# Left-factor sums of 35 block products built in DRAM by accumulating DMAs instead of on VectorE

## The chip, the cores and the metric

The kernel runs on one core of one Trainium2 chip. The metric is the device time of one execution in microseconds; a lower time is better. Three runs of the kernel before gave 2456.99, 2461.78 and 2462.23 us, median 2461.78. One more execution was recorded by the hardware profiler; it took 2457.39 us on the device, and the trace of it spans 2455.6 us.

## The reference, cut to what matters

One pre-norm layer on a sequence of 1024 rows of width 1024, in float32, then a last norm. Cut to its data flow:

```python
h = rmsnorm(x)
u = h @ w_in                      # 1024 x 11264, cut into dq, dk, dv, rq, rk, rv, rg, lx, ly, gates
od = diff_attention(dq, dk, dv)   # 8 heads, two softmaxes each, causal
o_r = silu(rg) * group_norm(retention(rq, rk, rv))
o_l = rg_lru(lx) * gelu(ly)       # convolution, gates, a scan over time
g = sigmoid(gates)                # three gates of width 1024
merged = g[0] * (od @ w_branch[0]) + g[1] * (o_r @ w_branch[1]) + g[2] * (o_l @ w_branch[2])
x = x + merged @ w_out
x = x + cross_attention(rmsnorm(x), rmsnorm(mem))
x = x + square(relu(rmsnorm(x) @ mlp_w1)) @ mlp_w2
return rmsnorm(x)
```

## The kernel before, in words

Every matmul operand is split into a high and a low part (`split`, lines 68 to 72: ScalarE writes the rounded high part, VectorE or GpSimd subtracts it for the low part), and one product is three matmuls (`mm3`, lines 57 to 61). So each operand costs a pass of ScalarE and one of VectorE or GpSimd before TensorE can use it.

The stages follow each other: retention (to about 262 us in the trace), attention (to about 740), `h_products` (to about 1220), three calls of `branch` (to about 1490), w_out and cross-attention, and the two matrix products of the MLP.

The products with `rg`, `lx` and `ly`, most of `gates`, the three w_branch matrices and mlp_w1 are made by a Strassen-like scheme with seven block products in place of eight (Winograd's form). Two rows of blocks of the left factor (here the weights) form a *pair*: `A11 A12` lie in one 128x1024 unit in DRAM, `A21 A22` in the next. The seven left operands are A11, A12, A22 and four sums, S1 = A21 + A22, S2 = S1 - A11, S3 = A11 - A21, S4 = A12 - S2 (`LEFT`, line 1058). The right operands are B11, B21, B22 and T1 to T4, which are made once and kept in SBUF as split blocks. There are 35 such pairs from the attention's end to the end of the third branch: 4 of `rg`, 8 of `lru`, 11 of `gate` in `h_products`, and 12 in the branches. mlp_w1 has 16 more, which the change leaves as they are.

For each pair `raw_pair` loads the two units on the SyncE queue (SP), `left` makes the four sums with four VectorE instructions of 128x512 (line 1066), in place over the loaded blocks, and `product` (lines 1103 to 1137) does the seven products of 12 matmuls each: `pair_unit` splits the left operand (ScalarE, then GpSimd or VectorE), the product goes into one PSUM bank, and VectorE adds the seven results up in the running sums `t0` and `t1` (lines 1125, 1127 and 1130) and in `emit`. The in-place sums must wait until the splits that read the old blocks are done. `h_products` and `branch` have six PSUM banks for these products (`p6`). In `h_products` the work of the LRU (convolution, line 615; scan, line 640) and the right-factor sums of the branches (`o_sums`, lines 739 to 750) run on the same VectorE queue.

In the attention stage each of the 8 heads has 8 steps of scores, softmax, transposes and products with v; the projections of the next heads fill in between. Their weights come through `weight` (lines 83 to 92): a 512 KB load on SP into one of three staging tiles, the high part on ScalarE, the low part on GpSimd, into one of four tiles `w`. The half of each q tile that lies on the other partitions is written by a DMA from SBUF to SBUF on the SP queue (`qd<-qd`, line 443), which the head's scores wait for.

The Python code writes the instructions in program order; a list scheduler puts them into one in-order queue for each engine, so an instruction can stand earlier or later than in the code. `after(key, ins)` chains instructions of one key in program order ("wdma" for weight loads, "wsplit" for their high parts). Each DMA on a queue also takes one of eight completion semaphores in turn.

Of the kernel before, what the change touches and what calls it, by code (L numbers as in the profile page):

```python
# [17 lines left out]
P = 128  # L18
# [31 lines left out]
class Kernel:  # L50
# [85 lines left out]
    def setup(self):  # L136
# [231 lines left out]
    def h_sums(self, kt, half, hp):  # L368
# [13 lines left out]
        for o, a, b in ((T2, B22, T1), (T4, B21, T2)):  # L382
            self.after("ret", tt(o, a[0], b))
            tt(o, o, a[1], ALU.add)
        nc.sync.dma_start(self.hTs[:, :, kt, c].rearrange("i p c -> p i c"), t[:, 0:4, :])
# [159 lines left out]
    def attention(self):  # L545
        self.vd, self.qkd, self.am = {}, {}, {}
        for _ in self.diff_v(0):
            pass
# [15 lines left out]
        for h in range(8):  # L564
# [25 lines left out]
        self.hp = self.h_products()  # L590
        for f in late:
# [55 lines left out]
    def h_products(self):  # L647
# [11 lines left out]
        sums = {4: [(0, 0)], 6: [(1, 0), (1, 1)], 8: [(1, 2), (1, 3)], 10: [(0, 1), (0, 2)], 12: [(0, 3)],  # L659
                14: [(2, 0), (2, 1)], 18: [(2, 2)], 20: [(2, 3)]}  # L660

        def run(p, k):
# [6 lines left out]
            elif kind == "rg":  # L669
                units = [a["w_rg"][2 * n + i] for i in range(2)]  # L670
            else:
                units = [a["w_gate"][self.gate_order[n + i]] for i in range(2)]

            def emit(i, j, x, y):
# [22 lines left out]
            psum = (lambda: self.ps.tile([P, HB], F32, tag="mm", name="ps1")) if k == 1 and p < 2 else None  # L697
            self.pair(p, k, c, units, H, psum or self.p6(sps), emit, nc.gpsimd)
            if kind == "lru" and k == self.ORDER[5]:
# [8 lines left out]
            if k == self.ORDER[2]:  # L708
                for i, q in sums.get(p, ()):
                    self.o_sums(i, q, sp)  # L710
# [28 lines left out]
    def o_sums(self, i, q, sp):  # L739
# [6 lines left out]
        (b11, b12), (b21, b22) = ([x[:, j, :] for j in range(2)] for x in t)  # L746
        for o, x, y in ((b11, b12, b11), (b12, b22, b12), (b22, b22, b11), (b21, b21, b22)):
            nc.vector.tensor_tensor(o, x, y, op=ALU.subtract)
        for e in range(2):
            nc.sync.dma_start(dst[2 * e:2 * e + 2, :, q, :].rearrange("i p c -> p i c"), t[e])  # L750

    def o_in(self, i):
# [39 lines left out]
    def branch(self, order, i, right, bw, st, sps, nxt):  # L792
# [25 lines left out]
        def run(p, k):  # L818
            units = [self.a["w_br"][i * 8 + 2 * p + e] for e in range(2)]
            self.pair(p, k, cs[p], units, right, self.p6(sps), lambda e, j, x, y: emit(2 * p + e, j, x, y),  # L820
                      v if k in (6, 4) else nc.gpsimd)
# [259 lines left out]

    def pair(self, p, k, c, units, right, psum, emit, lo):
# [5 lines left out]
        if "left" not in c and 1 in c and 2 in c:  # L1088
            c["left"] = True
            w = c["w"]  # L1090
            self.left(w, self.sf[:, 4 + p % 2, :], w["A11"], w["A12"], self.nc.vector)
        self.product(k, c, right, psum, lo, emit)

# [8 lines left out]

    def product(self, k, c, right, psum, lo, emit):

# [21 lines left out]
        if ready("u3", 7, "u2"):  # L1126
            v.tensor_tensor(t1, c[7], t0, op=ALU.add)
        if ready("c22", 5, "u3"):
            emit(1, 1, c[5], t1)
            v.tensor_tensor(t0, c[5], t0, op=ALU.add)  # L1130
        if ready("c21", 4, "u3"):
# [152 lines left out]
    def run(self):  # L1284
        tc, nc, a = self.tc, self.nc, self.a
        pool = lambda name, bufs=1, side="right", **kw: tc.tile_pool(name=name, bufs=bufs, side=side, reuse_waits="tile", **kw)
        self.setup()
        with pool("slotA", bufs=4, side="left") as self.slotA:
            self.n_gates, self.gate_order = 0, [b * 8 + n for b in (1, 0, 2) for n in range(8)]
# [108 lines left out]
```

## Time and profile before

| | |
|---|---|
| runs, median (lowest to highest) | 2461.78 us (2456.99 to 2462.23) |
| profiled execution, device time | 2457.39 us |
| its span in the trace | 2455.6 us |
| TensorE (PE) busy | 2320.9 us, 95% |
| weight loads of TensorE (PEld) busy | 1908.8 us, 78% |
| VectorE (DVE) busy | 1854.2 us, 76% |
| ScalarE (ACT) busy | 1044.8 us, 43% |
| GpSimd (POOL) busy | 1091.8 us, 44% |
| DMA, moved | 338.28 MB, mean 138 GB/s |

In the profile an engine's row gives busy time, not useful time: matmuls are pipelined, and a busy TensorE at a lower granted clock (PEclk) does less. "A <- B" among the waits reads: A's engine sat idle until B had ended. PE rows count matmuls; at full clock 88 to 90 matmuls of 128x512 fit into 20 us. L numbers are lines of the kernel before.

### The profile page before, as it was taken

How to read it: one execution, taken by the hardware profiler on the slowest of the kernel's cores; microseconds unless marked ns; L12 is line 12 of the kernel's file. 1: busy time of each engine (PE TensorE's matmuls, PEld its weight loads, DVE VectorE, ACT ScalarE, POOL GpSimd, SP SyncE). 2: the span in 40 equal slices, each digit the busy share in tenths (PEclk: the TensorE clock that was granted, in tenths of full speed). 3: DMA queues.
4: the chain of work that ended last, by engine and by line, in shares of the span. 5: the costliest groups of instructions: out<-in, count | busy, mean ns of one | idle time of the engine just before them, and what ended most of it. 6: DMA issues, size and time to landing. Idle time of an engine off the chain costs nothing. (4 is left out here: it accounts for less than half of the span.)

```text
span 2455.6 us, 31231 instructions
## 1 busy us (share of the span) xinstructions
PE 2320.9 (95%) x11132; PEld 1908.8 (78%) x11132; DVE 1854.2 (76%) x2850; ACT 1044.8 (43%) x1823; POOL 1091.8 (44%) x714
## 2 busy tenths in 40 slices
PE   9999999999998999999998987999989999999996
PEld 7888878888876877777876766788768888778884
DVE  7677387877786776786677898345788888788888
ACT  5444355555545454445244443135432222343333
POOL 1122212221216555566542334034155555698787
PEclk9999999999999999999999988999999999999999
DMA  4222222222225345453676776343325444734431
GB/s 170 80 86 70 65 61 69 66 64 62 61 56 195 119 162 171 140 178 112 208 252 211 256 263 193 112 162 104 106 80 175 150 156 141 274 138 172 158 138 74
DMA packets 137259, 338.28 MB, mean 138 GB/s; under 512 B 17152, under 2 KB 27393, under 8 KB 137104
## 3 DMA queue, kind: packets, MB, share of 16 engines
q1 hardware_dynamic: 136528, 334.44, 41.4%
q8 instruction: 89, 1.46, 0.2%
q10 hardware_dynamic: 576, 1.84, 0.2%
q14 instruction: 66, 0.54, 0.1%
HBM read 229.21 MB, written 98.63 MB: 134 GB/s over the span
## 5 line engine op out<-in xcount | busy, mean ns | idle before, releaser
L59 PE MATMUL ps<-block,wu 128*128 128x512 f32 x1428 | 570.7, 400 | 53.8 <-DVE sf L1125 21.5
L61 PE MATMUL ps<-block,wu 128*128 128x512 f32 x1428 | 567.8, 398 | 11.4 <-POOL wu L71 6.2
L60 PE MATMUL ps<-block,wu 128*128 128x512 f32 x1428 | 564.4, 395 | 1.7 <-POOL block L71 1.0
L71 POOL TENSOR_TENSOR wu<-st,wu 128x512 fp32r<-128x512 f32 x214 | 323.3, 1525 | 317.5 <-ACT wu L70 317.4
L59 PEld LDWEIGHTS ps<-block,wu 128*128 128x128 f32 x1428 | 272.9, 191 | 118.1 <-issue 19.5
L61 PEld LDWEIGHTS ps<-block,wu 128*128 128x128 f32 x1428 | 272.8, 191 | 79.2 <-POOL wu L71 11.0
L60 PEld LDWEIGHTS ps<-block,wu 128*128 128x128 f32 x1428 | 272.9, 191 | 62.8 <-DVE block L71 1.6
L70 ACT CAST wu<-st 128x512 fp32r<-128x512 f32 x240 | 141.2, 618 | 166.6 <-DVE st L1066 71.3
L71 POOL TENSOR_TENSOR w<-st,w 128x1024 fp32r<-128x1024 f32 x50 | 123.7, 2485 | 158.3 <-ACT w L70 158.2
L59 PE MATMUL ps<-wu,hu 128*128 128x512 f32 x448 | 177.2, 395 | 17.1 <-DVE acc L1198 14.3
L61 PE MATMUL ps<-wu,hu 128*128 128x512 f32 x448 | 174.8, 392 | 3.6 <-DVE hu L71 3.6
L60 PE MATMUL ps<-wu,hu 128*128 128x512 f32 x448 | 175.5, 392 | 0.0
L1198 DVE TENSOR_TENSOR acc<-acc,ps 128x512 f32<-128x512 f32 x216 | 137.8, 678 | 20.4 <-PE ps L61 19.9
L71 POOL TENSOR_TENSOR wu<-sf,wu 128x512 fp32r<-128x512 f32 x63 | 116.7, 1866 | 67.9 <-ACT wu L70 57.3
L71 DVE TENSOR_TENSOR hu<-sth,hu 128x1024 fp32r<-128x1024 f32 x56 | 121.1, 2167 | 20.9 <-ACT hu L70 20.2
L466 ACT ACTIVATE p<-sc,mx 128x256 f32<-128x256 f32 (+7 forms) x128 | 94.8, 741 | 71.1 <-DVE mx L463 49.2
L59 PEld LDWEIGHTS ps<-wu,hu 128*128 128x128 f32 x448 | 84.7, 189 | 41.3 <-DVE acc L1198 12.4
L61 PEld LDWEIGHTS ps<-wu,hu 128*128 128x128 f32 x448 | 84.7, 189 | 22.6 <-DVE hu L71 4.9
L59 PE MATMUL psk<-block,w 128*128 128x512 f32 x256 | 101.7, 397 | 0.0
L61 PE MATMUL psk<-block,w 128*128 128x512 f32 x256 | 101.2, 395 | 0.0
L60 PE MATMUL psk<-block,w 128*128 128x512 f32 x256 | 100.8, 394 | 0.0
L60 PEld LDWEIGHTS ps<-wu,hu 128*128 128x128 f32 x448 | 84.7, 189 | 17.2 <-POOL wu L71 0.4
(389 smaller groups left out, 5608.0 us busy)
## 6 DMA issues: line engine op xcount, KB each, us to landing
sth<-h SPq DMA_DIRECT2D x56, 512.0 KB, 9.4
st<-in_w SPq DMA_DIRECT2D x32, 512.0 KB, 4.3
h<-hab SPq DMA_DIRECT2D x32, 512.0 KB, 2.8
w<-in_w SPq DMA_DIRECT2D x8, 2048.0 KB
sgb<-gsp SPq DMA_DIRECT2D x48, 256.0 KB, 4.4
gsp<-l SPq DMA_DIRECT2D x44, 256.0 KB, 2.1
acc<-y SPq DMA_DIRECT2D x40, 256.0 KB, 3.8
st<-in_w_br SPq DMA_DIRECT2D x18, 512.0 KB, 5.5
```

Source lines behind the costliest of these rows:

```text
L59: nc.tensor.matmul(ps, lhsT=lhs.hi, rhs=rhs.hi, start=start, stop=False)
L60: nc.tensor.matmul(ps, lhsT=lhs.hi, rhs=rhs.lo, start=False, stop=False)
L61: nc.tensor.matmul(ps, lhsT=lhs.lo, rhs=rhs.hi, start=False, stop=stop)
L70: ins = self.nc.scalar.copy(dst.hi, src)
L71: self.lo_ins = (lo_engine or self.nc.vector).tensor_tensor(dst.lo, src, f32(dst.hi), op=ALU.subtract)
L466: nc.scalar.activation(p[:, 0:n], sc[:, 0:n], AF.Exp, bias=mx, accum_out=l)
L1198: eng.tensor_tensor(acc[k][:, st, :], acc[k][:, st, :], x if isinstance(x, bass.AP) else acc[x][:, st, :], op=ALU.add)
```

## The change

The four sums of each of the 35 pairs are no longer made on VectorE. A generator, `left_sums`, makes them in DRAM in nine batches of three or four pairs. One yield of it is taken at each of the first steps of the attention's 64, until it is exhausted (54 steps), with two batches taken in turn. In each batch: two plain copies on SP (into S1 and S3), two accumulating DMAs issued by GpSimd (which add a weight block in DRAM to the copy in DRAM), a copy S1 to S2, an add to S2, a copy S2 to S4, an add to S4. A DMA moves 128 x 4 x 512 elements, 1 MB (three pairs: 0.75 MB). An accumulating DMA can only add, so the form is changed to one without subtractions on the left: S1 = A21 + A22, S3 = A11 + A21, S2 = S1 + A11, S4 = S2 + A12; the signs of the right sums (`h_sums`, `o_sums`) and of three of the output sums (`positive` in `product`) are changed to fit, with as many VectorE instructions as before.

`pair` then loads what it needs as it goes: A11 and A12 in one load, A22 alone (256 KB), S2 with S1, and S4 with S3. That is four loads and 1.75 MB for a pair, where it was two and 1 MB. Three of the four go through the three staging tiles. During the attention the accumulating DMAs and the low parts of the weights are chained on GpSimd in program order (key "sumadd"), and the copies and the weight loads on SP (key "wdma").

```diff
@@ weight
         self.after("wsplit", self.split(s, st, lo or self.nc.gpsimd))
+        if self.summing:
+            self.after("sumadd", self.lo_ins)
@@ setup
+        self.lsum = {k: self.dram.tile([n, 2, P, 2, HB], F32, name="ls_" + k) for k, n in (("rg", 4), ("lru", 8), ("gate", 12), ("br", 12))}
@@ attention
             for i in range(8):
                 advance()
+                next(self.lsums, 0)
                 self.diff_scores(h, i)
@@ new
+    def left_sums(self):
...
+        def batch(key, n0, n1):
+            w, order = src[key]
+            A = lambda i, j: w[n0:n1, order[i - 1], :, (j - 1) * HB:j * HB].rearrange("n p c -> p n c")
+            S = {k: self.lsum[key][n0:n1, g, :, x, :].rearrange("n p c -> p n c")
+                 for k, (g, x) in {1: (0, 1), 2: (0, 0), 3: (1, 1), 4: (1, 0)}.items()}
+            copy = lambda o, x: self.after("wdma", nc.sync.dma_start(o, x))
+            add = lambda o, x: self.after("sumadd", nc.gpsimd.dma_start(o, x, accum_op=ALU.add))
+            copy(S[1], A(2, 1))
+            copy(S[3], A(1, 1))
+            yield
+            add(S[1], A(2, 2))
+            add(S[3], A(2, 1))
+            yield
+            copy(S[2], S[1])
+            yield
+            add(S[2], A(1, 1))
+            yield
+            copy(S[4], S[2])
+            yield
+            add(S[4], A(1, 2))
+            yield
+
+        todo = [("rg", 0, 4), ("lru", 0, 4), ("gate", 5, 8), ("lru", 4, 8), ("gate", 0, 4), ("gate", 8, 12),
+                ("br", 4, 8), ("br", 0, 4), ("br", 8, 12)]
...
@@ pair
         if k == 1:
-            st = self.sf[:, 6:8, :].rearrange("p k c -> p (k c)") if p % 2 else None
-            c["w"] = self.raw_pair(units, st)
...
-            self.left(w, self.sf[:, 4 + p % 2, :], w["A11"], w["A12"], self.nc.vector)
...
+        name, w = self.LEFT[k], c["w"]
+        if name not in w:
+            if k == 1 and p > 1:
+                st = self.sf[:, 4 + 2 * (p % 2):6 + 2 * (p % 2), :].rearrange("p k c -> p (k c)")
+            else:
+                st = self.stage.tile([P, D], F32, tag="st", name="st")
...
+            self.after("wdma", self.nc.sync.dma_start(st, src))
@@ product
         if ready("u3", 7, "u2"):
-            v.tensor_tensor(t1, c[7], t0, op=ALU.add)
+            if positive:
+                v.scalar_tensor_tensor(t1, c[7], -1.0, t0, op0=ALU.mult, op1=ALU.subtract)
```

The order of three queues shows what moves. First GpSimd at the end of the retention stage (`rsr` and `mv` are the scales of its last rows, `ks` a low part of a key; `w` are low parts of the attention's weights, `mc` the first row scale of the attention's output). Before:

```order
L71 TENSOR_TENSOR w<-st,w 128x1024 x2
L71 TENSOR_TENSOR ks<-qk,ks 128x128
L97 TENSOR_TENSOR rsr<-rsr,mhalf 128x1
L312 TENSOR_SCALAR mv<-mv,rsr 128x1
L97 TENSOR_TENSOR rsr<-rsr,mhalf 128x1
L312 TENSOR_SCALAR mv<-mv,rsr 128x1
```

The same place on GpSimd of the changed kernel (L774 is an accumulating DMA, `ls_` a tensor of sums in DRAM):

```order
L71 TENSOR_TENSOR w<-st,w 128x1024 x2
L774 DMA ls_rg<-in_w_rg 128x4x512
L71 TENSOR_TENSOR ks<-qk,ks 128x128
L99 TENSOR_TENSOR rsr<-rsr,mhalf 128x1
L774 DMA ls_rg<-in_w_rg 128x4x512
L316 TENSOR_SCALAR mv<-mv,rsr 128x1
L99 TENSOR_TENSOR rsr<-rsr,mhalf 128x1
L774 DMA ls_lru<-in_w_lru 128x4x512
```

The first adds stand behind the second of the attention's weights and between the retention's last scales. Later, 35 of the 36 adds stand ahead of the low part of the first weight for head 7's projections.

Next SP, from the end of retention to the first q tiles of head 0 (`onT` are stores of retention, `in_w_dqk` and `in_w_dv` weight loads of the attention). Before:

```order
L86 DMA st<-in_w_dqk 128x1024 x2
L325 DMA onT<-ost 128x2x256 x3
L86 DMA st<-in_w_dv 128x1024 x2
L86 DMA st<-in_w_dqk 128x1024
L443 DMA qd<-qd 64x1024 x3
```

The same stretch of SP in the changed kernel (L773 is a plain copy in DRAM):

```order
L773 DMA ls_rg<-ls_rg 128x4x512
L329 DMA onT<-ost 128x2x256
L773 DMA ls_lru<-ls_lru 128x4x512
L329 DMA onT<-ost 128x2x256
L86 DMA st<-in_w_dqk 128x1024
L773 DMA ls_rg<-ls_rg 128x4x512
L773 DMA ls_lru<-ls_lru 128x4x512
L86 DMA st<-in_w_dqk 128x1024
L86 DMA st<-in_w_dv 128x1024 x2
L773 DMA ls_gate<-in_w_gate 128x3x512
L448 DMA qd<-qd 64x1024 x4
```

Four copies, each of which waits for an accumulating DMA, now stand ahead of the first `qd<-qd`; the second two wait for adds that GpSimd issues behind weights of the attention.

Last VectorE in an LRU pair of `h_products` (`sf` holds the running sums, `lx` and `l` the results, `g<-r,xc` is the scan). Before:

```order
L1127 TENSOR_TENSOR sf<-ps_9743,sf 128x512
L639 TENSOR_TENSOR xc<-xc,g 128x1024
L1066 TENSOR_TENSOR st<-st 128x512
L640 SCALAR_TENSOR_TENSOR g<-r,xc 128x1024
L675 TENSOR_TENSOR lx<-ps_9760,sf 128x512
L641 TENSOR_TENSOR l_9334<-l_9334,g 128x1024
L1130 TENSOR_TENSOR sf<-ps_9760,sf 128x512
```

The same pair in the changed kernel:

```order
L1192 SCALAR_TENSOR_TENSOR sf<-ps_9814,sf 128x512
L646 TENSOR_TENSOR xc<-xc,g 128x1024
L647 SCALAR_TENSOR_TENSOR g<-r,xc 128x1024
L683 TENSOR_TENSOR lx<-ps_9831,sf 128x512
L648 TENSOR_TENSOR l_9409<-l_9409,g 128x1024
L1198 TENSOR_TENSOR sf<-sf,ps_9831 128x512
```

The in-place sum ahead of the scan is gone; the rest stands in the same order.

More of the change, by code (lines that the diff above doesn't have):

```diff
@@ L381, in h_sums @@
             tt(o, o, x, ALU.add)
-        for o, a, b in ((T2, B22, T1), (T4, B21, T2)):
-            self.after("ret", tt(o, a[0], b))
-            tt(o, o, a[1], ALU.add)
+        self.after("ret", tt(T2, T1, B22[0]))
+        tt(T2, T2, B22[1])
+        self.after("ret", tt(T4, B21[0], T2, ALU.add))
+        tt(T4, T4, B21[1], ALU.add)
         nc.sync.dma_start(self.hTs[:, :, kt, c].rearrange("i p c -> p i c"), t[:, 0:4, :])
@@ L708, in run @@
             if k == self.ORDER[2]:
-                for i, q in sums.get(p, ()):
+                for i, q in osums.get(p, ()):
                     self.o_sums(i, q, sp)
@@ L746, in o_sums @@
         (b11, b12), (b21, b22) = ([x[:, j, :] for j in range(2)] for x in t)
-        for o, x, y in ((b11, b12, b11), (b12, b22, b12), (b22, b22, b11), (b21, b21, b22)):
-            nc.vector.tensor_tensor(o, x, y, op=ALU.subtract)
+        for o, x, y in ((b11, b12, b11), (b12, b22, b12), (b22, b11, b22), (b21, b21, b22)):
+            nc.vector.tensor_tensor(o, x, y, op=ALU.add if o is b21 else ALU.subtract)
         for e in range(2):
             nc.sync.dma_start(dst[2 * e:2 * e + 2, :, q, :].rearrange("i p c -> p i c"), t[e])
+    def left_sums(self):
+        nc, a = self.nc, self.a
+        pairs = lambda w: w.rearrange("(n e) p c -> n e p c", e=2)
+        src = {"rg": (pairs(a["w_rg"]), (0, 1)), "lru": (a["w_lru"], (1, 0)), "gate": (pairs(a["w_gate"]), (0, 1)),
+               "br": (pairs(a["w_br"]), (0, 1))}
+        def batch(key, n0, n1):
[21 more added lines that the diff above has]
+                ("br", 4, 8), ("br", 0, 4), ("br", 8, 12)]
+        todo, run = [batch(*t) for t in todo], []
+        while todo or run:
+            while todo and len(run) < 2:
+                run.append(todo.pop(0))
+            b = run.pop(0)
+            if next(b, 0) is None:
+                run.append(b)
+                yield
     def o_in(self, i):
```

39 lines of the change are left out of this document (28 added, 11 removed).

## The prediction

> **What bounds the kernel now.** I read the page's first part, then the windows by stage, then TensorE's waits in the stages with pairs, then the timelines around its stalls. First the page, then four windows (start and end, length, then busy time and instruction count of PE, PEld, DVE, ACT, POOL, then granted clock, DMA share, GB/s): attention, `h_products` after its first 40 us, and the branches up to and around the third one's start.
>
> ```profile
> PE 2320.9 (95%) x11132; PEld 1908.8 (78%) x11132; DVE 1854.2 (76%) x2850; ACT 1044.8 (43%) x1823; POOL 1091.8 (44%) x714
> 300.00:740.00 440.00, 430.87 (x2544) 365.70 (x2544) 347.12 (x709) 231.61 (x488) 95.72 (x68) 1.00 0.25 65
> 780.00:1220.00 440.00, 418.58 (x1765) 336.97 (x1766) 326.98 (x361) 207.29 (x299) 254.24 (x164) 0.98 0.47 157
> 1220.00:1320.00 100.00, 96.77 (x421) 78.20 (x419) 73.51 (x81) 45.09 (x67) 40.95 (x25) 1.00 0.70 233
> 1320.00:1420.00 100.00, 80.06 (x338) 65.01 (x338) 84.30 (x100) 45.61 (x68) 34.46 (x22) 0.91 0.76 250
> ```
>
> TensorE is the bound everywhere, so the change can win only what TensorE idles, and the slow clock behind it, in the pairs' stages. Attention idles 9 us of 440. Who ends the idle time from 740 to 1492 us (total, times, longest):
>
> ```profile
> PE ps L59 <- DVE sf L1125: 21.5, 4, 10.3
> PE ps L59 <- DVE sf L1130: 15.2, 6, 2.6
> PE ps L61 <- POOL wu L71: 6.2, 10, 1.1
> ```
>
> The six L1130 stalls lie in LRU pairs of `h_products`, the L1125 ones in the branches. In both VectorE frees a PSUM bank late. One LRU pair, VectorE and then TensorE:
>
> ```profile
> 942.71 1.76 DVE L1066 TENSOR_TENSOR st<-st 128x512 f32<-128x512 f32 x1 [1.16 <-POOL wu L71]
> 944.39 3.38 DVE L640 TENSOR_TENSOR_SCAN g<-r,xc 128x1024 f32<-128x1024 f32 x1
> 947.70 0.66 DVE L675 TENSOR_TENSOR lx<-ps,sf 128x512 f32<-128x512 f32 x1
> 948.28 1.65 DVE L641 TENSOR_TENSOR l<-l,g 128x1024 f32<-128x1024 f32 x1
> 949.85 0.68 DVE L1130 TENSOR_TENSOR sf<-ps,sf 128x512 f32<-128x512 f32 x1
> ...
> 947.66 0.40 PE L61 MATMUL ps<-block,wu 128*128 128x512 f32 x1
> 950.67 0.50 PE L59 MATMUL ps<-block,wu 128*128 128x512 f32 x1 [2.61 <-DVE sf L1130]
> ```
>
> The left sum L1066 first waits 1.16 us for GpSimd (it overwrites a block that GpSimd still reads), runs 1.76, and pushes the scan and the freeing L1130 back.
>
> **What goes: the sums on VectorE.** L1066 alone in 740 to 1492 us, two 20 us windows side by side, and the 3.8 us behind that stall:
>
> ```profile
> 740.00:1492.00 752.00, 135.79 (x137) 0.00 (x0) 0.97 0.57 189
> 920.00:940.00 20.00, 20.00 (x89) 16.43 (x88) 11.53 (x16) 13.35 (x16) 9.68 (x7) 1.00 0.47 152
> 940.00:960.00 20.00, 16.26 (x64) 12.57 (x63) 18.81 (x19) 6.38 (x12) 11.29 (x7) 0.91 0.34 116
> 950.60:954.40 3.80, 3.73 (x10) 2.94 (x11) 3.76 (x6) 0.00 (x0) 0.46 (x1) 0.55 0.85 276
> ```
>
> 136 us of VectorE work leave these stages, but not off the path one for one. In the pair above, 1.16 + 1.76 = 2.9 us less ahead of L1130 is more than the stall of 2.61. At full clock a matmul takes 20/89 = 0.225 us; the ten at a clock of 0.55 took 3.8 us where 2.25 would do, so each stall drags 1.5 us of slow clock behind it. Six stalls: 15.2 + 6 x 1.5 = 24 us. What is late next there is GpSimd's low part, 6.2 us in ten pieces, which stays. I count **-24 us**; bounds: 0, if other work fills the place, and the whole deficit of the window 780 to 1220, 440/0.225 = 1956 matmuls against 1765, 191 x 0.225 = 43 us.
>
> In the branches, the end of an 8.46 us stall and of the longest, in VectorE's rows:
>
> ```profile
> 1324.60 1.75 DVE L1066 TENSOR_TENSOR sf<-st 128x512 f32<-128x512 f32 x1
> ...
> 1327.79 0.69 DVE L1125 TENSOR_TENSOR sf<-ps,sf 128x512 f32<-128x512 f32 x1
> ...
> 1416.34 1.75 DVE L1066 TENSOR_TENSOR sf<-st 128x512 f32<-128x512 f32 x1
> ...
> 1418.73 0.68 DVE L1125 TENSOR_TENSOR sf<-ps,sf 128x512 f32<-128x512 f32 x1
> ```
>
> Without the sums L1125 comes 3.2 and 2.4 us earlier, 5.6 us. The rest of both stalls is the loading of the next right blocks, which stays. Against that stand the branches' extra loads: 12 pairs x 0.75 MB = 9 MB. By the rows below that is 29 us of the DMA engines in a stage already at 0.70 to 0.76; a tenth of it on the path takes back 3 us. **-3 us** (+10 to -12).
>
> **What comes: 72 transfers in the attention.** Volume: 35 pairs x 4 x 0.262 MB = 36.7 MB by copies and as much by adds. No accumulating DMA, and no transfer with both ends in DRAM, is in this trace. The nearest rows are the busiest 20 us of the DMA engines, the attention's own traffic, and the landing times of a 1 MB and a 512 KB transfer:
>
> ```profile
> 1360.00:1380.00 20.00, 20.00 (x89) 16.43 (x88) 16.06 (x22) 8.14 (x15) 9.46 (x7) 1.00 0.87 288
> 240.00:590.00 350.00, 340.33 (x2037) 292.77 (x2036) 252.64 (x555) 174.35 (x368) 80.86 (x59) 1.00 0.25 65
> acc<-x SPq DMA_DIRECT2D x4, 1024.0 KB, 10.1
> h<-hab SPq DMA_DIRECT2D x32, 512.0 KB, 2.8
> ```
>
> 288 GB/s at a share of 0.87 is 331 GB/s; 1.05 MB take 3.2 us of all engines. An add reads twice and writes once, so I take two passes, 6.4 us; bounds are one pass, 3.2, and the 1 MB row, 10.1. The Trainium skill says the same of the reducing primitive in "Collectives: The Full Stack", Part 3: two source reads, half the rate of a copy; no run here shows it.
>
> They cost nothing while they stay ahead of what is queued behind them. Adds block GpSimd, and the attention's low parts of weights stand behind; copies wait on SP for adds, with weight loads and q tiles behind. The cover is the lead of these:
>
> ```profile
> 248.89 4.87 POOL L71 TENSOR_TENSOR w<-st,w 128x1024 fp32r<-128x1024 f32 x2 [2.41 <-ACT w L70]
> 284.26 4.76 POOL L71 TENSOR_TENSOR w<-st,w 128x1024 fp32r<-128x1024 f32 x2 [20.73 <-ACT w L70]
> 595.90 2.40 POOL L71 TENSOR_TENSOR w<-st,w 128x1024 fp32r<-128x1024 f32 x1 [1.35 <-ACT w L70]
> 637.86 0.48 PE L59 MATMUL psk<-block,w 128*128 128x512 f32 x1
> 302.25 1.81 SPq L443 DMA_DIRECT2D qd<-qd  x2
> ```
>
> First, head 0's q tiles. The first add can go at 248.9 + 4.9 = 254 us. Four adds are queued; the third (LRU's S1) is through at 254 + 19 + 1 = 274, its copy to S2 at 278. The S2 adds stand behind the two low parts of 284 to 289 us, so both end at 289 + 13 = 302, and the S4 copy that waits for the second goes at 302, `qd<-qd` at 303 against 302.25. With adds of 10.1 us it is 311. I take **+3 us** (0 to 9).
>
> Second, the whole. The low part made at 595.90 is the first of head 7's projections, used at 637.86, a lead of 42 us; 35 adds stand ahead of it. From 254 to 637.9 - 2.4 = 635 us are 381 us, and some 13 more since the last two adds need only be issued: 394. Needed: adds 36.7/0.331 x 2 = 222 us, copies 111 less the four already done (13), 98 us, the attention's own 65 GB/s x 381 us = 25 MB, 75 us; together 395. That just fits, without the gaps between dependent transfers; I put those at **+7 us**. Adds at one pass leave 110 us to spare; each us more than 6.4 for an add costs some 35 us. GpSimd's own time to issue an add is not in the trace: SP's issues take 0.3 to 0.5 us, a low part of a weight 2.4; 36 of either hide in the 344 us that GpSimd idles in the attention. Near 254 us adds stand between the retention's last scales, but products with v fill in there; taken as 0 (to 8).
>
> **What moves in the pairs.** Four loads instead of two, three of them through three staging tiles:
>
> ```profile
> DMA to landing us min/median/max: 3.5/4.3/6.5
> ```
>
> The tile of S4 and S3 is free after the seventh product's split and needed at the next pair's fourth; between lie three products, 36 x 0.225 = 8.1 us, against 4.3 for the load and about 2 for the splits: hidden, unless SP holds the load behind a store. The sign changes swap an instruction for one of the same size. Cost 0.
>
> **Sum.** -24 - 3 + 3 + 7 = -17 us, on the profiled execution 2457.4 - 17 = 2440; that execution lies 4.4 under the median, so against 2461.8 it is **2444 us**.
>
> **The rivals.**
> The sums outrun their cover (slower): DRAM-to-DRAM transfers go slower than loads from DRAM to SBUF, SP and GpSimd block, and TensorE waits for weights and q tiles. For it: the account above is full at 6.4 us an add, and the 1 MB row says 10.1. Against it: the 42 us lead, and 10.1 was under other traffic. It decides from about 6.9 us an add, where 17 us are gone; at 8 us the time is 2444 + 56 = 2500, at 10.1 about 2444 + 130 = 2574. Chance 0.31. "DMA: Bandwidth & Descriptors", Latency and other measured facts, in the Trainium skill gives 207 to 214 GB/s in each direction for copies between HBM tensors; an estimate from it is 5.0 us a copy, 64 us more in all, 2508 us.
>
> The loads take the sums' place (about no change): the staging tiles or SP's order make splits wait, half a us a pair, 35 x 0.5 = 17 us, and 2444 + 17 = 2461. For it: SP is in order, and the branches' DMA share of 0.76. Against: 8.1 us of slack. Chance 0.13.
>
> More than counted (faster): with VectorE some 136 of 752 us freer, the deficit in `h_products` (43 us) goes nearly whole and adds take one pass: -43 - 5 + 0 = -48, 2414 us. Chance 0.07.
>
> **How the numbers follow.** My forecast, 0.49, has its own range of 2426 (attention free, branches -12) to 2458. 0.2%, 4.9 us, is about what a measurement of this kernel can tell from no change; 2457 to 2467 counts as the same, so 0.02 of the forecast's 0.49 falls there with most of the loads' 0.13, of which 0.02 is slower. Faster 0.47 + 0.07 = 0.54, same 0.13, slower 0.33. The range runs from 2414 to 2515, where an add costs 8.4 us; beyond it lie half of the last case and 0.13 of the first.
>
> **What would show it.** Right: no L1066 from the attention's end to 1490 us, L1130's heirs gone from TensorE's waits, a granted clock of 1.00 in most 20 us windows of `h_products`, attention ending within 12 us of before, its DMA share near 1. Wrong: waits of TensorE on `w` or `qd` in the attention with SP or GpSimd waiting for DMAs of `ls_`; or ScalarE's `wu` waiting for `st<-ls_` in the pairs.

## The result, and the profile after

| | before | after |
|---|---|---|
| median (lowest to highest) | 2462.01 us (2456.99 to 2462.33) | 2559.01 us (2558.24 to 2559.76) |
| span of the profiled execution | 2455.6 us | 2557.8 us |

The ratio is 1.0397, 95% interval 1.0381 to 1.0414: 97 us slower. One execution of e5 below took 3791.9 us at a granted clock of 0.555, where its others took 2569.5 to 2573.8, and is left out of its median. The page of the changed kernel, its engines and its two large DMA queues (SyncE's, then GpSimd's; packets, MB, share of the span):

```profile
PE 2341.3 (92%) x11132; PEld 1921.3 (75%) x11132; DVE 1767.2 (69%) x2710; ACT 1047.8 (41%) x1823; POOL 1123.0 (44%) x750
q1 hardware_dynamic: 165104, 398.68, 46.5%
q0 software_dynamic: 18496, 36.70, 8.2%
```

VectorE has 140 instructions and 87 us less: its sums are gone. GpSimd's queue is new: the 36 adds moved 36.7 MB in 8.2% of 2557.8 = 210 us of all 16 DMA engines, 6.0 us for 1.05 MB. Where the time went is read from the attention's softmax, first and last exponential, before and after:

```profile
L466 ACT ACTIVATE p<-sc,mx x128: 351/741/1121, 307.1 to 731.6; 128x128 f32<-128x128 f32 x16, 128x256 f32<-128x256 f32 x16, 128x384 f32<-128x384 f32 x16, 128x512 f32<-128x512 f32 x16
```

```profile
L471 ACT ACTIVATE p<-sc,mx x128: 363/740/1122, 320.4 to 851.0; 128x128 f32<-128x128 f32 x16, 128x256 f32<-128x256 f32 x16, 128x384 f32<-128x384 f32 x16, 128x512 f32<-128x512 f32 x16
```

The attention starts 13 us late and ends 119 us late; the span is 102 us longer, so the pairs' stages win 17 back. The windows that answer to those of before (attention, `h_products`, branches), in the same columns:

```profile
320.00:760.00 440.00, 347.34 (x1990) 296.66 (x1989) 278.39 (x545) 177.91 (x374) 108.16 (x79) 0.88 0.75 181
890.00:1330.00 440.00, 423.03 (x1808) 338.98 (x1807) 276.70 (x285) 210.58 (x305) 257.83 (x170) 0.99 0.60 200
1330.00:1430.00 100.00, 96.78 (x412) 77.96 (x411) 58.12 (x67) 49.74 (x72) 38.42 (x26) 0.98 0.83 284
```

In the attention TensorE idles 93 us of 440 where it idled 9, and its clock falls to 0.88; the DMA share is 0.75, not near 1. TensorE's waits there (240 to 860 us), then behind it (860 to 1610):

```profile
PE ms L522 <- ACT s L70: 42.7, 7, 16.8
PE sc L463 <- ACT p L471: 30.5, 7, 15.2
PE sc L463 <- DMA qd<-qd: 10.9, 2, 10.6
...
PE ps L59 <- DVE sf L1189: 13.3, 4, 6.4
PE ps L61 <- POOL wu L71: 12.6, 17, 1.5
PE ps L59 <- ACT wu L70: 8.2, 7, 3.8
```

The longest one, followed back through four engines, says how. `mc`, `rows` and `rb` belong to the chain of a row scale: four small transfers (`rows<-sq`, `mc<-rows`, `rows<-mc`, `rb<-rows`) around two GpSimd instructions, then the product `od`. GpSimd, SyncE, ScalarE, TensorE:

```profile
562.19 1.03 POOL L541 TENSOR_TENSOR mc<-mc,mhalf 128x4 f32<-128x4 f32 x1
571.57 1.33 POOL L774 DMA_DIRECT2D ls_br<-in_w_br  x1 [8.35 <-DMA ls_br<-in_w_br]
591.34 1.25 POOL L547 TENSOR_TENSOR od<-od,rb 128x512 f32<-128x512 f32 x1 [18.44 <-DMA rb<-rows]
...
552.50 1.52 SPq L773 DMA_DIRECT2D ls_br<-in_w_br  x2
563.25 0.33 SPq L542 DMA_DIRECT2D rows<-mc  x1
563.62 0.56 SPq L773 DMA_DIRECT2D ls_br<-in_w_br  x1
581.99 0.33 SPq L545 DMA_DIRECT2D rb<-rows  x1
...
592.63 0.60 ACT L517 ACTIVATE sq<-oT 128x512 f32<-128x512 f32 x1 [16.35 <-POOL od L547]
...
593.93 0.79 PE L522 MATMUL ms<-s,onesr 128*128 128x512 f32 x1 [16.77 <-ACT s L70]
```

SyncE sends the row scale at 563.25, but the transfer that spreads it over the partitions goes only at 581.99, 18.7 us later, and lands at 591.2; only then can GpSimd multiply. What SyncE waits for is the landing of `rows<-mc`, 2 KB. Such waits over the attention, in the changed kernel (240 to 860 us) and in the one before (240 to 740):

```profile
SPq L545 <- DMA rows<-mc: 38.5, 12, 17.7
```

```profile
SPq L540 <- DMA rows<-mc: 16.9, 12, 2.8
```

Ahead of `rows<-mc` in SyncE's queue stand the two copies of 1 MB sent from 552.50 on. By the trace's semaphore updates, which mark that a DMA is done, they land at 570.88 and 581.01, and `rows<-mc` at 581.93; `rb<-rows` lands at 591.20, behind the copy of 563.62, which lands at 589.22. So both small transfers came in right behind the copies ahead of them. `rb` and ScalarE's next squares `sq` share one tile, so ScalarE stands with all that is queued behind it, and TensorE idles 16.77 us. The same two transfers in the kernel before, KB each and median us from issue to landing:

```profile
rb<-rows SPq DMA_DIRECT2D x15, 256.0 KB, 4.0
...
rows<-mc SPq DMA_DIRECT2D x15, 2.0 KB, 2.4
```

6.4 us then, 28 us here (563.3 to 591.2).

### The profile page after: what moved, and what is told of

It is laid out like the page before. It is cut to its first block, busy times and chain, and to the rows that moved or that the text cites. A ratio compares the mean times of both kernels' runs of the same rounds, so it can differ in the third digit from the quotient of the medians.

```text
span 2557.8 us, 31356 instructions
## 1 busy us (share of the span) xinstructions
PE 2341.3 (92%) x11132; PEld 1921.3 (75%) x11132; DVE 1767.2 (69%) x2710; ACT 1047.8 (41%) x1823; POOL 1123.0 (44%) x750
## 3 DMA queue, kind: packets, MB, share of 16 engines
q0 software_dynamic: 18496, 36.70, 8.2%
## 5 line engine op out<-in xcount | busy, mean ns | idle before, releaser
L71 POOL TENSOR_TENSOR wu<-st,wu 128x512 fp32r<-128x512 f32 x223 | 351.4, 1591 | 304.9 <-ACT wu L70 298.4
L70 ACT CAST wu<-st 128x512 fp32r<-128x512 f32 x255 | 149.2, 618 | 175.3 <-PE ps L61 77.1
L463 PE MATMUL sc<-kd,qd 128*128 128x512 f32 (+3 forms) x384 | 101.2, 382 | 41.6 <-ACT p L471 30.5
L59 PEld LDWEIGHTS ps<-wu,hu 128*128 128x128 f32 x448 | 84.7, 189 | 41.2 <-DVE acc L1268 12.5
L463 PEld LDWEIGHTS sc<-kd,qd 128*128 128x128 f32 x384 | 69.3, 206 | 57.5 <-ACT p L471 37.5
L59 PE MATMUL psk<-block,w 128*128 128x512 f32 x256 | 104.4, 408 | 7.3 <-DVE qd L447 7.3
L71 POOL TENSOR_TENSOR wu<-sf,wu 128x512 fp32r<-128x512 f32 x54 | 79.0, 1476 | 70.9 <-ACT wu L70 64.9
L61 PE MATMUL psk<-block,w 128*128 128x512 f32 x256 | 103.5, 404 | 0.0
L60 PE MATMUL psk<-block,w 128*128 128x512 f32 x256 | 103.2, 403 | 0.0
```

Of the source, the lines that this page charges most:

```text
L59: nc.tensor.matmul(ps, lhsT=lhs.hi, rhs=rhs.hi, start=start, stop=False)
L60: nc.tensor.matmul(ps, lhsT=lhs.hi, rhs=rhs.lo, start=False, stop=False)
L61: nc.tensor.matmul(ps, lhsT=lhs.lo, rhs=rhs.hi, start=False, stop=stop)
L70: ins = self.nc.scalar.copy(dst.hi, src)
L71: self.lo_ins = (lo_engine or self.nc.vector).tensor_tensor(dst.lo, src, f32(dst.hi), op=ALU.subtract)
L463: nc.tensor.matmul(sc[:, b * HB:b * HB + e], lhsT=qt[:, c, part, cols], rhs=k[b][:, c, 0:e], start=part == 0, stop=part == 1)
```

## Theories and experiments

T1: in-order queues. SyncE's copies wait for adds, GpSimd's adds for copies, and weights, q tiles and row scales stand behind them. T2: the bytes fill the DMA engines, whoever waits. T3: GpSimd is what blocks, by issuing the adds or waiting in them. Rival A, formed after the first four runs: SyncE's own queue, where small transfers stand behind 1 MB ones.

The medians, the ratio to the kernel before, measured beside each run, with its interval, and the last exponential of the attention in the profiled execution (before: 731.6). The kernel before had medians from 2458.5 to 2465.8 us beside the different groups of runs, so a difference of two medians from different groups is good to some 5 us:

| run | what | us | ratio | last exp |
|---|---|---|---|---|
| e1 | no transfers of sums | 2446.0 | 0.9944 (0.9928 to 0.9960) | 731.1 |
| e7 | 36 copies, SyncE | 2446.2 | 0.9946 (0.9930 to 0.9962) | 741.6 |
| e15 | 72 copies, SyncE | 2456.0 | 0.9966 (0.9947 to 0.9985) | 748.3 |
| e8 | e3, half the bytes | 2461.9 | 1.0003 (0.9986 to 1.0020) | 755.5 |
| e10 | e3, adds as plain copies | 2490.5 | 1.0110 (1.0085 to 1.0135) | 782.0 |
| e16 | e10 without waits | 2495.7 | 1.0127 (1.0102 to 1.0153) | 782.0 |
| e2 | no dependent copies or adds | 2518.9 | 1.0249 (1.0232 to 1.0266) | 813.6 |
| e3 | no copy waits for an add | 2522.4 | 1.0258 (1.0232 to 1.0284) | 811.3 |
| e6 | e3, all 72 on GpSimd | 2524.6 | 1.0254 (1.0220 to 1.0288) | 814.7 |
| after | | 2559.0 | 1.0397 (1.0381 to 1.0414) | 851.0 |
| e5 | copies in a chain of their own | 2571.8 | 1.0458 (1.0441 to 1.0476) | 863.6 |

**e1_no_sums.**

```diff
-        todo, run = [batch(*t) for t in todo], []
+        todo, run = [], []
...
-                    src, got = sums[g].rearrange("p k c -> p (k c)"), ("S4", "S3") if g else ("S2", "S1")
+                    src, got = units[g], ("S4", "S3") if g else ("S2", "S1")
```

> The 72 transfers of sums in the attention are left out; each pair still makes its four loads, of the same bytes, but S1 to S4 get raw weight blocks in place of sums, so the output's products are others. It measures what the pairs' stages win when the attention is untouched. Both theories (T1: the loss is in-order waits for the transfers; T2: the loss is the transfers' bytes) put the whole loss into the attention: its last exponential at about 732 us as before, and the time 2462 - 17 = 2445 us, range 2435 to 2455, since the changed kernel is 119 us late at the end of attention and 102 late at the end. If the pairs' loads cost something of their own that the attention hid, it is 2455 or more.

2446.0 us, attention as before. So the whole loss lies with the 72 transfers, 113 us, and the pairs' stages win 0.56%, some 14 us. The same 760 us of both kernels, before and e1:

```profile
740.00:1500.00 760.00, 705.59 (x2990) 567.50 (x2990) 579.09 (x653) 356.24 (x522) 383.09 (x244) 0.97 0.57 190
```

```profile
740.00:1500.00 760.00, 715.98 (x3055) 574.05 (x3054) 488.58 (x533) 365.28 (x529) 379.53 (x246) 0.98 0.68 230
```

65 matmuls more at 0.225 us are 14.6 us: the same answer.

**e2_no_chain and e3_copies_free.** e2, then e3:

```diff
-            copy(S[2], S[1])
+            copy(S[2], A(1, 1))
...
-            add(S[2], A(1, 1))
+            add(S[2], A(2, 1))
...
-            copy(S[4], S[2])
+            copy(S[4], A(1, 2))
...
-            add(S[4], A(1, 2))
+            add(S[4], A(1, 1))
```

```diff
-            copy(S[2], S[1])
+            copy(S[2], A(1, 1))
...
-            add(S[2], A(1, 1))
+            add(S[2], S[1])
...
-            copy(S[4], S[2])
+            copy(S[4], A(1, 2))
...
-            add(S[4], A(1, 2))
+            add(S[4], S[2])
```

> The same 72 transfers with the same bytes on the same queues, but none reads what another of its batch has written: S2 starts as a copy of A11 and gets A21, S4 starts as a copy of A12 and gets A11 (so S2 and S4 lack terms and the output's products are others). A copy never waits for an add; an add waits only for its own copy. T1 (SP and GpSimd stand still in program order behind dependent transfers, with weight loads, q tiles and row scales queued behind): most of the 119 us goes, the time is 2445 to 2480 us. T2 (bytes and their contention delay the small transfers, whoever waits): the bytes are the same, the time stays at 2530 to 2560. Between: a mixture, in proportion.

> The same sums, bytes and queues, with the operands of two steps exchanged: S2 = copy of A11, then S1 added; S4 = copy of A12, then S2 added. No copy on SP waits for an add any more, the three adds of a batch that depend on one another remain, and wait on GpSimd. T1 with SP as the queue that blocks: 2450 to 2490 us. T3 (it is GpSimd that blocks: adds wait for adds with the row scales mc and the products od queued behind): stays at 2530 to 2560. T2 (bytes): stays at 2540 to 2560.

2518.9 and 2522.4: both between the theories. Copies that wait for adds cost 37 us of the 113; adds that wait for adds cost nothing that can be told. 76 us remain with T2, T3 or rival A.

**e5_unchained.**

```diff
-            copy = lambda o, x: self.after("wdma", nc.sync.dma_start(o, x))
+            copy = lambda o, x: self.after("lcopy", nc.sync.dma_start(o, x))
```

> The changed kernel, with the copies on SP in a chain of their own in place of the chain of the weight loads, so that the scheduler may put weight loads ahead of copies that wait. Same sums, bytes and transfers. T1 with the weight loads as what suffers on SP: 20 to 60 us of the 97 go, 2500 to 2540. T2 (bytes) and T3 (GpSimd blocks): no change, 2550 to 2565.

A miss for all: 2571.8 us, 13 us slower than the changed kernel. The place in the chain of the weight loads is not what hurts.

**e6_pool_ring.** The edit stands in e3:

```diff
-            copy = lambda o, x: self.after("wdma", nc.sync.dma_start(o, x))
+            copy = lambda o, x: self.after("sumadd", nc.gpsimd.dma_start(o, x))
```

> The sums in the order of e3_copies_free (2522 us), with the 36 copies issued by GpSimd too, so that SyncE's queue holds none of the 72 transfers; the same bytes. Rival A: SyncE's queue is what delays q tiles and weights (they stand behind 1 MB copies in their own queue, and take a completion semaphore that a copy of eight transfers before still holds): q tiles land in 3 to 4 us as before (median 2.9), against 7.2 in e3, waits of TensorE on them go from 46 us to below 10, and the time falls to 2480 or less, unless GpSimd's blocking grows by as much, which its waits would show. Rival B (T2: the DMA engines are shared, whoever issues): q tiles still land in 6 us or more, the time stays at 2510 to 2540.

No change against e3, but for another reason. TensorE's waits in e3, then in e6 (240 to 860 us):

```profile
PE sc L463 <- DMA qd<-qd: 46.3, 5, 22.6
PE ms L522 <- ACT s L70: 19.5, 5, 12.1
```

```profile
PE ms L522 <- ACT s L70: 52.1, 7, 14.9
...
PE sc L463 <- DMA qd<-qd: 4.4, 1, 4.4
```

The waits on q tiles go, as A said; waits on squares behind GpSimd's `od` take their place, as ScalarE's waits in e6 show (18.4 us in e3):

```profile
ACT sq L517 <- POOL od L547: 43.5, 5, 12.3
```

Each queue has its own victims.

**e7_copies_only and e8_half.** Both edits stand in e3; e8's pairs also load raw blocks, as in e1:

```diff
-            add = lambda o, x: self.after("sumadd", nc.gpsimd.dma_start(o, x, accum_op=ALU.add))
+            add = lambda o, x: None
```

```diff
-            A = lambda i, j: w[n0:n1, order[i - 1], :, (j - 1) * HB:j * HB].rearrange("n p c -> p n c")
+            A = lambda i, j: w[n0:n1, order[i - 1], 0:64, (j - 1) * HB:j * HB].rearrange("n p c -> p n c")
-            S = {k: self.lsum[key][n0:n1, g, :, x, :].rearrange("n p c -> p n c")
+            S = {k: self.lsum[key][n0:n1, g, 0:64, x, :].rearrange("n p c -> p n c")
```

> e3_copies_free without its 36 adds (the sums lack their second terms, so the output's products are others): the copies' 36.7 MB on SyncE's queue alone, half the bytes, by the account (3.2 us for a copy, 6.0 for an add, of all engines) a third of the engines' time. Rival A (SyncE's queue): the copies stand there as in e3, 46 us of q waits stay in good part, 2475 to 2500 us. T2 (share of the engines): 2446 (e1_no_sums) plus at most a third of e3's 76, below 2470. T3 (GpSimd's blocking): 2446 to 2450.

> e3_copies_free with the 72 transfers cut to 64 of 128 partitions: half the bytes, the same number of transfers, waits and places in the queues; the pairs load raw blocks of the same size (the output's products are others). T2 and rival A alike (a transfer is late by the bytes ahead of it): the 76 us above e1_no_sums fall to half or less, 2450 to 2484 us, and q tiles land in under 5 us. If the number of transfers and of their waits were the cost, whatever their bytes: 2505 or more.

The copies alone cost nothing in the median (10 us in the attention of the profiled execution, which was a longer one, 2453.1 us). Half the bytes with all waits and places in the queues cost 16 us where the whole cost 76. So it is not the count of transfers, and the loss grows faster than the bytes.

**e10_plain, e15_sp_only, e16_pool_nowait.** e10, then e15, both against e3; e16 is e15 with `nc.gpsimd` and "sumadd" in its third line:

```diff
-            add = lambda o, x: self.after("sumadd", nc.gpsimd.dma_start(o, x, accum_op=ALU.add))
+            add = lambda o, x: self.after("sumadd", nc.gpsimd.dma_start(o, x))
```

```diff
+            Z = {k: self.lsum2[key][n0:n1, g, :, x, :].rearrange("n p c -> p n c")
...
+            add = lambda o, x: self.after("wdma", nc.sync.dma_start(o, x))
...
-            add(S[1], A(2, 2))
-            add(S[3], A(2, 1))
+            add(Z[1], A(2, 2))
+            add(Z[3], A(2, 1))
...
-            add(S[2], S[1])
+            add(Z[2], A(2, 2))
...
-            add(S[4], S[2])
+            add(Z[4], A(2, 1))
```

> e3_copies_free (2522 us) with its 36 adds on GpSimd issued without the accumulation, as plain copies of the same source to the same place (so the sums lack their first terms and the output's products are others). The number of transfers, their queues, their waits and their bytes as written stay; an add took 5.9 us of all engines per MB and a copy 3.0, so the engines' time for the sums falls from 304 to about 212 us. T2 (the engines' time): most of the 76 us above e1_no_sums goes, 2455 to 2485 us, q tiles land in 5 us or less. T3 (it is GpSimd's issue, its own queue and its blocking): 2510 to 2525.

> The bytes of e10_plain (2490.5 us) with no wait between transfers: 72 plain copies, the second 36 into a tensor of their own that nobody reads, all on SyncE (the sums lack their second terms, so the output's products are others). T2 (the engines' time, some 212 us of it as in e10, whoever issues): 2480 to 2495. T3 (GpSimd's issue and its waits made e10's 44 us): 2446 to 2456, as 36 such copies did. Rival A (SyncE's queue): at or over 2490.

> As e15_sp_only, but the second 36 copies issued by GpSimd, still with no wait for any other transfer. Against e10 only GpSimd's waits for the first copies are gone, against e15 only the queue differs. T2: 2480 to 2495, all three alike. T3 with the waits as the cause: 2446 to 2460, well below e10. T3 with the issue as the cause: as e10, 2490, and e15 well below.

By these three T2 falls as it was put, by the bytes whoever sends them. Same bytes: 2456.0 on one queue, 2495.7 on two, 2490.5 on two with waits. First e15, then e16, over the attention and over the 20 us in which head 0 starts:

```profile
250.00:740.00 490.00, 468.90 (x2758) 401.06 (x2758) 355.92 (x756) 240.61 (x511) 109.26 (x81) 0.98 0.63 190
300.00:320.00 20.00, 17.03 (x74) 13.48 (x73) 9.29 (x27) 6.53 (x17) 2.34 (x1) 0.91 0.96 317
```

```profile
250.00:740.00 490.00, 439.39 (x2592) 376.89 (x2592) 333.87 (x699) 223.52 (x474) 129.46 (x110) 0.95 0.61 195
300.00:320.00 20.00, 8.06 (x36) 6.49 (x35) 2.06 (x3) 3.30 (x5) 3.64 (x3) 0.76 1.04 324
```

The landing of copies that SyncE sends in both, those 24 of the 36 that leave from 300 to 620 us, e15 and then e16:

```profile
DMA to landing us min/median/max: 6.4/8.4/16.3
```

```profile
DMA to landing us min/median/max: 8.0/15.3/20.7
```

The engines are as busy in both (0.63 and 0.61 over the attention, full in the 20 us), and TensorE makes 166 matmuls more in e15. With a second queue sending at the same time these copies land in 15.3 us instead of 8.4 (the second copies of the pairs, in the same window: 12.4 from SyncE in e15, 12.0 from GpSimd in e16). The q tiles behind them land in up to 16.0 instead of up to 7.3, though their medians are alike, 6.0 and 6.4 (the view has the landing of some of them only). T3 falls as it was put: without its waits (e16) GpSimd costs as much as with them (e10), and TensorE waits in e16 for q tiles, not for GpSimd:

```profile
PE sc L464 <- DMA qd<-qd: 29.4, 3, 11.9
```

What comes before the longest of these stalls in e16, on SyncE, on GpSimd and on TensorE:

```profile
290.68 1.23 SPq L776 DMA_DIRECT2D ls_gate<-in_w_gate  x2
291.95 3.85 SPq L776 DMA_DIRECT2D ls_lru<-in_w_lru  x2
299.91 0.33 SPq L86 DMA_DIRECT2D st<-in_w_dqk  x1
302.65 0.52 SPq L449 DMA_DIRECT2D qd<-qd  x1
...
290.19 0.74 POOL L777 DMA_DIRECT2D l_lru<-in_w_lru  x1
299.82 0.74 POOL L777 DMA_DIRECT2D l_rg<-in_w_rg  x1
300.55 0.74 POOL L777 DMA_DIRECT2D l_lru<-in_w_lru  x1
...
319.35 0.66 PE L464 MATMUL sc<-kd,qd 128*128 128x128 f32 x2 [11.94 <-DMA qd<-qd]
```

In e15 SyncE sends the same transfers from 289.89 on, and one copy more ahead of the q tile; yet by the semaphore updates the tile sent at 302.71 lands there at 310.3, and the one sent at 302.65 here lands at 319.2. So this stall does not come of another order on SyncE; what is left, by the two traces, are GpSimd's three copies in flight beside it. In e15 their like had left SyncE earlier, from 208 us on: the second queue changes when the bytes move, too, and how much of the 40 us is due to either was not taken apart. The Trainium skill's "DMA: Bandwidth & Descriptors", SWDGE vs HWDGE vs iDMA, says that GpSimd's and SyncE's transfers feed different queues in each DMA engine, which takes them in turn; the landing times do not contradict that, and no run here shows the turns.

From e10 to e3 only the accumulation differs: 32 us.

```profile
q0 software_dynamic: 9536, 36.70, 4.3%
```

That is e10's GpSimd queue; e3's reads 8.2%. 4.3% of 2489.9 us is 3.06 us for 1.05 MB, 8.2% of 2517.3 is 5.90. The Trainium skill's "Collectives: The Full Stack", Part 3, has half the rate of a copy for a reduction, for its second read; the rates here agree (3.06 against 5.90 us, with 9536 packets against 18496), and no run tells whether the second read is the reason.

**e12_local, e13_pool_local, e14_nosums_local.** The same line in the changed kernel, in e6 and in e1:

```diff
-        if (h, half) == (7, 1):
+        if True:
```

> The changed kernel with the same 72 transfers, but the 15 row scales of the attention's output are made as the last one is already: on ScalarE over the whole tile (identity, logarithm, exponential, 128x512 each) and one multiplication on VectorE, in place of four small transfers, two instructions and a multiplication on GpSimd. So nothing of the row scales waits for a transfer or for GpSimd. T1 (the chain of the row scales, late behind the sums, holds ScalarE through the tile it shares with the next squares): the 43 us of TensorE's waits on `s` go and part of the 30 us on `p`, less some 10 us for the new work: 2500 to 2535. T2 (the engines are full; another late transfer takes the place): 2545 to 2565.

> e6_pool_ring (2525 us; all 72 transfers on GpSimd, TensorE's waits: 52 us on `s`, 4 on q tiles) with the row scales made locally as in e12_local. T1: with the chain gone and SyncE's queue free, nothing late is left on the path but weights whose low parts stand behind adds on GpSimd: 2524 - 52 = 2472, 2465 to 2495 us. T2: the same traffic in the same engines moves the waits elsewhere: 2510 or more.

> e1_no_sums (2446 us; no transfers of sums, pairs load raw blocks, so the output's products are others) with the row scales made locally as in e12 and e13: the price of the local form by itself, which those two pay too. If it is small (15 times some 2 us of ScalarE beside other work): 2446 to 2455 us, and e13 still loses 50 us and more to the transfers, whatever holds. If it is 20 us or more: 2466 to 2480, then e13 (2504) loses only 25 to 40 to the transfers where e6 lost 79, and the chain of the row scales was a main path.

2551.6 (ratio 1.0359, 1.0333 to 1.0385), 2504.3 (1.0164, 1.0137 to 1.0191) and 2487.6 us (1.0091, 1.0070 to 1.0113). By e12 alone T1 would have fallen; e14 shows why not: the local form itself costs 41.6 us against e1 (36 by the two ratios). With that price on both sides the transfers cost 2551.6 - 2487.6 = 64 us in the changed kernel instead of 113, and 17 in e6 instead of 79. In the attention of e13 the DMA share is 0.79, above the changed kernel's 0.75, and still TensorE idles only 53 us of 490, where it idles 34 in e14, which has no sums, and 93 of 440 in the changed kernel (e13, then e14):

```profile
250.00:740.00 490.00, 437.14 (x2537) 371.51 (x2536) 340.09 (x695) 268.04 (x513) 137.71 (x107) 0.97 0.79 200
```

```profile
250.00:740.00 490.00, 455.61 (x2661) 387.04 (x2660) 338.93 (x734) 278.68 (x540) 67.78 (x37) 0.98 0.20 54
```

So the chain of the row scales carries up to 49 of the 113 us, and up to 62 of e6's 79; some of that fall may be that the longer attention leaves the transfers more room.

**Attempts at a faster kernel.** The main lines of their edits, in this order. e9: sums in DRAM for the 8 LRU pairs alone. e11: for the 23 pairs of `h_products`, begun in the retention stage. e17: e6 with four batches in turn and `od` on VectorE. e18: e17 for the 23 pairs.

```diff
-        todo = [("rg", 0, 4), ("lru", 0, 4), ("gate", 5, 8), ("lru", 4, 8), ("gate", 0, 4), ("gate", 8, 12),
-                ("br", 4, 8), ("br", 0, 4), ("br", 8, 12)]
+        todo = [("lru", n, n + 2) for n in range(0, 8, 2)]
```

```diff
         def step(t):
+            if t > 3 and t % 2:
+                next(self.lsums, 0)
```

```diff
-            while todo and len(run) < 2:
+            while todo and len(run) < 4:
-        nc.gpsimd.tensor_tensor(od, od, rb, op=ALU.mult)
+        nc.vector.tensor_tensor(od, od, rb, op=ALU.mult)
```

```diff
-                next(self.lsums, 0)
+                if h > 0 and (h + i) % 3:
+                    next(self.lsums, 0)
```

> Only the 8 LRU pairs get their sums in DRAM (23% of the bytes), in four batches of two pairs with the order of e3, so 16 copies and 16 adds of 0.5 MB, one at every second of the attention's 64 steps; the other 27 pairs make the same all-additions sums on VectorE, with the loads of before. If bytes in flight are the cause, the attention loses at most 5 us (last exponential at 732 to 737), while the six stalls of LRU pairs in the products go: 24 us by the old account, but the 35 pairs together won only 12 to 16 (e1_no_sums), so 2446 to 2460 against 2459 to 2462 before. If each transfer costs by its count, the attention loses 32/72 of 80 us, 35: 2480 or more.

> The sums of the 23 pairs of h_products alone (66% of the bytes), in the order of e3, begun in the retention stage (its DMA share was 0.1 to 0.3, and TensorE waits for none of its transfers): 16 of the 36 steps there, one at every second step, the rest at every third step of the attention; the 12 pairs of the branches make the same sums on VectorE with the loads of before. If the engines' time in the attention is the cause: the attention ends 5 to 12 us late instead of 80, and with the win of the products (some 15) the time is 2448 to 2462, at or below before. If adds cost by GpSimd's blocking, the retention's scales wait behind them and the retention ends late by 10 us or more: 2465 or more.

> All sums, and all their 72 transfers on GpSimd as in e6_pool_ring (2525 us), but with four batches taken in turn in place of two (so that GpSimd waits less for a transfer's landing), and the multiplication of the attention's output by its row scales on VectorE in place of GpSimd. If the loss goes by what stands behind the transfers on GpSimd and not by the bytes: e13 lost 17 us against e14, which has the same price of the local scales, so 2446 + 17 = 2463, and up to 30 more for the row scales' power, which stays on GpSimd: 2463 to 2495. If the second read of the adds counts by itself (30 us between e10 and e3): 2495 or more.

> e17 with the sums of the 23 pairs of h_products alone (66% of the bytes), begun after head 0 and spread over two of three steps; the 12 pairs of the branches make the all-additions sums on VectorE with the loads of before. If the loss goes by the transfers in flight: a third to a half of e17's loss less, at the price of the branches' small win (3 us): 2453 to 2475, beside 2459 to 2463 before. If it is no better than e17, the loss goes by the places in GpSimd's queue and not by the amount.

None beats the kernel before: 2480.0 us (1.0072, 1.0055 to 1.0088), 2503.2 (1.0160, 1.0137 to 1.0182), 2549.2 (1.0340, 1.0317 to 1.0362) and 2523.2 (1.0234, 1.0211 to 1.0257). In e9 the attention ends 8 us late, 3 more than expected, and the products win nothing: the other 10 us are lost there, where its LRU pairs need more staging tiles (argued, not tried). In e11 the attention takes 14 us more, and the retention stage ends 40 us late; TensorE and ScalarE from 40 to 350 us:

```profile
PE tpo L324 <- ACT on L317: 32.6, 7, 18.7
...
ACT on L317 <- POOL mv L316: 63.4, 29, 6.4
```

There the retention's scales stand between the adds on GpSimd. e17 took `od` from GpSimd, and the late `rb` then held VectorE instead (240 to 860 us):

```profile
DVE od L547 <- DMA rb<-rows: 80.7, 12, 16.8
```

So the late transfer cost where its reader stood in order, and moving the reader moved the cost, as far as e17 tells, which changed two things at once. e18, with two thirds of the bytes, loses 26 us less than e17.

## Why the prediction was wrong, point by point

**The sums' removal, -27 us:** right in kind, half in size. e1 gives 14, and L1130's heir (L1198) nearly left TensorE's waits (15.2 us before, 4.0 in e1). The rest went to the rival that the prediction called loads in the sums' place: waits of TensorE on `wu` from ScalarE and GpSimd, 7.3 us before (1.1 and 6.2), are 18.0 in e1 (8.5 and 9.5), 10.7 us more. ScalarE's own waits there, in e1, name the loads:

```profile
ACT wu L70 <- DMA st<-in_w_br: 25.8, 17, 5.0
...
ACT wu L70 <- DMA st<-in_w_gate: 21.3, 5, 7.1
```

The step on the four loads, "hidden" and "Cost 0", failed by these 11 us; that the loads cause them is read from the waits, and no run took the loads away.

**The price of transfers:** right. Taken: 6.4 us an add, 3.2 a copy. Measured: 5.9 to 6.0 and 3.1. The estimate of 5.0 us a copy, from the 207 to 214 GB/s of "DMA: Bandwidth & Descriptors" in the Trainium skill, was too high for the rows here: e15 moved 317 GB/s in the 20 us shown, some q tiles among it.

**Head 0's q tiles, +3 us:** 13 measured.

**The whole, +7 us: the step that failed.** "They cost nothing while they stay ahead of what is queued behind them", and "the cover is the lead", with a lead of 42 us from one low part to TensorE's use of it. By volume the account held for plain copies: 72 of them cost 10 us on SyncE's queue (5 by the ratios); accumulating transfers were not run on that queue. But a lead to TensorE's use is no cover where an in-order engine that TensorE needs meanwhile reads the transfer. The row scales have no such lead: late by 20 us they hold GpSimd's `od`, ScalarE's `sq` and TensorE at once. They were counted among the attention's 65 GB/s, not as a chain of four transfers that land behind whatever copies are in flight ahead of them in SyncE's queue, as in the stall above. Forecast for the attention were 10 us (3 + 7), and 113 were lost. These 113 us (after over e1), from run to run in this order: bytes 10 (e15 over e1), half of them moved to a second queue 34 to 40 (e10 and e16 over e15), the accumulation 27 to 32 (e3 over these), copies that wait for adds 37 (after over e3).

**The rival "the sums outrun their cover"** had the direction and the place, and not the mechanism: it was to decide from 6.9 us an add, and adds at 6.0 lost 113 us. The sign named for it, waits on `qd` with SyncE waiting for `ls_` DMAs, came, but in the changed kernel the row scales, which it did not name, were the longer part (42.7 us of waits on squares against 10.9 on q tiles); in e3 and e16 the q tiles were (46.3 against 19.5, and 29.4 against 7.6).

## What to carry to other kernels

Background transfers like these are costed by the small transfers they delay, not by their bytes against the engines' free time: list each transfer of the stage with the in-order engine that reads it, and count as cover only what that engine can wait before its next instruction is late. Here bulk copies cost least on the stage's own queue, with no transfer waiting for another (e15), and more when a second queue sent beside it (e16); with the accumulation they cost as much with all 72 on GpSimd's queue (e6) as with the copies on SyncE's (e3). Test a cure by its own price too: e12 looked like a refutation until e14 was run.

## What the runs showed of the hardware

- GpSimd took 0.745 us (median of the most frequent forms in e16) to issue a plain copy of 512 rows, and 1.3 to 1.5 us (medians of the forms in the changed kernel, at most 3.3) for an accumulating one.
- An accumulating DMA took about twice a copy's engine time, 5.90 against 3.06 us for 1.05 MB; in the changed kernel an add landed in 8.2, 13.6 and 31.4 us (least, median, most).
- At the same bytes and nearly the same DMA share over the attention (0.63 and 0.61), 72 copies on SyncE's queue cost 10 us, and half of them moved to GpSimd's, which also sent them later, 40 more.
- A transfer of 2 KB, sent behind two copies of 1 MB on the same queue, landed 0.9 us after the second of them and 18.7 us after it was sent; such a transfer landed in 2.4 us (median) in the kernel before.
